# HGRN2's values of all four heads in one 512-column product, computed behind the memory attention

## The chip, the core and the metric

The kernel runs on one core of a Trainium2 chip. A core has five engines that run their own instruction queues side by side: TensorE (PE; its weight loads are shown apart as PEld), VectorE (DVE), ScalarE (ACT), GpSimd (POOL), and SyncE (SP), which here only starts DMA transfers. Each queue is served in order: an instruction that waits holds up all that stand behind it on its engine. The metric is the time of one execution on the device, in microseconds (us), lower is better.

## The reference

One decoder layer over 1024 tokens of width 1024. One projection of the normalised input gives the columns for three groups of heads; their outputs are concatenated, projected, added, and followed by a SwiGLU block.

```python
h = rmsnorm(x, norm_mix[layer])
hq, hf, hi, hg, sq, sk, sv, iq, ik, iw, mq = split_in(h @ w_in[layer])
o_hg = hgrn2_mix(hq, hf, hi, hg, lb[layer], hg_out_gain[layer])        # 4 heads, state 128 x 128
o_sa = dsa_mix(sq, sk, sv, iq, ik, iw, sa_q_gain[layer], sa_k_gain[layer])  # top 256 keys of each query
o_mem = mem_mix(mq, mem_n, w_mem_kv[layer], mem_q_gain[layer], mem_k_gain[layer])  # 256 memory tokens
x = x + jnp.concatenate([o_hg, o_sa, o_mem], -1) @ w_out[layer]
a, b = jnp.split(rmsnorm(x, norm_ffn[layer]) @ w_ffn_in[layer], 2, axis=-1)
x = x + (jax.nn.silu(a) * b) @ w_ffn_out[layer]
```

The change touches `hi`, the values of the gated recurrence: 1024 tokens by 512 columns (4 heads of 128), a product of the normalised input with 1024 x 512 weights.

## The kernel before

Activations lie transposed: 128 channels on the partitions, tokens along the free axis. Every large product is done in float32 accuracy with three passes: both operands are split into a high part (fp32r) and the rest, and high x high, high x low and low x high are added in PSUM (`PASSES`, three pairs). A split of weights is one ACT copy (`whi`) and one subtraction (`wlo`), on POOL in this part of the program.

Weights come in pages of 512 KB, 1024 numbers a partition, through two staging buffers (tag `wst`, two of them for the whole program), and are split from there into tiles of 512 columns (tags `whi`, `wlo`, four of each). A staging buffer is free again when both of its halves are split.

Two shapes of projection stand in this part of the program:

- `proj` (its matmuls are line 184): a page of weights is the stationary operand, 512 tokens move. For a page of 128 outputs: 2 halves of the tokens x 8 slices of the channels x 3 passes = 48 matmuls of 512 columns. The two halves use the two banks of tag `mm`.
- `token_major` (line 453): 128 tokens are the stationary operand and 256 columns of weights move, so that the result has tokens on the partitions. For 256 outputs: 2 pages (each one half of the channels) x 8 tiles of tokens x 12 = 192 matmuls of 256 columns, accumulated in four banks (two of tag `lg`, two of tag `sm`) with two tiles of tokens in each bank; `scaled_rows` (line 462) writes them out with ACT, 8 copies of 128 x 256.

`hgrn_v(pair)` computes the values of two heads with `token_major`. It is called twice: pair 0 first of all, ahead of the memory attention, and pair 1 just before the state of head 1.

The stage around it, from the end of the index scores (about 150 us) to the queries of the sparse attention (about 517 us), holds much independent work at once:

- `memory_attention`: 8 blocks of queries x 2 pairs of heads. Each: logits (PE, line 686), maximum (DVE, 690), exponential (ACT, 693), scaling (POOL, 697), transposes (PE, 702), a copy (ACT 704 or DVE 706), values (PE, 711). It uses the banks `lg`, `rc` and `sm`, its queries `mqs` in x8 to x11, its keys `kms` in x6 and x7 and its values `vm` in x12.
- two searches for the 256th largest score of each query, 32 rounds each, every round one step deeper into the bits of the threshold: `bisect((7, 4), V)` counts on DVE (line 635: 1024 and 640 columns a round), `bisect((6, 5, 3, 2), S)` counts on ACT (line 632: 896, 768, 512 and 384 columns a round) and updates the threshold on DVE (lines 637, 647, 644, 627). A round can't begin before the round ahead of it has ended on DVE. Behind the last round the masks of those blocks are made: counting (657, 667), prefix sums (672) and combination (673, 674) on DVE, comparisons on POOL (669, 675).
- the four heads of the recurrence, for each `hgrn_proj` (3 pages, evacuated by DVE line 481), `hgrn_gates` (ACT lines 493, 495, 496, 501; DVE 494; POOL 497, 498, 502), `hgrn_intra` (six levels of fp32 products, PE line 511, each followed by DVE 521, 523, 535 and POOL 522, then two with line 542) and `hgrn_state` (PE 560, 567, 583, 585, 601).
- pages of queries, keys and values for the sparse attention (names `sap_`).

The program is written as calls in a row (memory attention, head 0, and so on), but a scheduler fixes the order on each engine when the kernel is built: it lists instructions as they become ready in its own timing of the program, within the limits that buffers and banks set. So the static order on PE and DVE interleaves the parts, and it changes wherever the program changes.

Of the kernel before, what the change touches and what calls it, by code (L numbers as in the profile page):

```python
# [42 lines left out]
def hybrid_block(ctx, tc, xT, memT, wch, wikw, wv, wkm, wvm, woa, wob, wfi, wfo,  # L43
                 vec, cst, lvl, out):
    nc = tc.nc
# [14 lines left out]
    def nm(p):  # L60
        cnt[0] += 1
        return f"{ph[0]}_{p}{cnt[0]}"
# [8 lines left out]
    def xt(i, shape, dt=F32):  # L71
        return xp.tile(shape, dt, tag=f"x{i}", name=nm(f"x{i}_"))

    def mt(i, shape=(128, 1024)):
        return mp.tile(list(shape), F32, tag=f"m{i}", name=nm(f"m{i}_"))
# [7 lines left out]
    def bs(b):  # L83
        return slice(b * 128, b * 128 + 128)
# [358 lines left out]
    def token_major(g0):  # L443

        acc = [bank("lg"), bank("lg"), bank("sm"), bank("sm")]
        for g in range(2):
            w = load_page(wv[g0 + g], 4, 256)
            for tt in range(8):
                o = acc[tt // 2][:, 256 * (tt % 2):256 * (tt % 2) + 256]
                i = 0  # L450
                for pw, p in PASSES:
                    for k in range(4):
                        T.matmul(o, H[p][4 * g + k][tt // 4][:, bs(tt % 4)], w(pw, k),
                                 start=g == 0 and i == 0 and tt % 2 == 0,
                                 stop=g == 1 and i == 11 and tt % 2 == 1)
                        i += 1
        return [a.rearrange("p (t d) -> p t d", t=2) for a in acc]

    def scaled_rows(dst, acc):

        for tt in range(8):
            S.activation(dst[tt // 4][:, tt % 4, :], acc[tt // 2][:, tt % 2, :], AF.Copy,
                         scale=rn[:, tt:tt + 1])

    def hgrn_v(pair):
        ph[0] = "hg"
        Vp = [xt(10 + j, [128, 4, 256]) if pair else mt(4 + j, (128, 4, 256)) for j in range(2)]
        scaled_rows(Vp, token_major(2 * pair))
        for j in range(2):
            Vh[2 * pair + j] = lambda c, j=j: Vp[c // 4][:, c % 4, bs(j)]  # L470

    def hgrn_proj(h):
        ph[0] = "hg"
# [131 lines left out]
    def run(steps):  # L605
        ph[0] = "hg"
        for _ in steps:
            pass
# [141 lines left out]

        proj(page(20), 128, H, evac_q0)

    hgrn_v(0)
    memory_attention()
    hgrn_proj(0)
    hgrn_gates(0)
    run(hgrn_intra(0))
    hgrn_proj(1)
    hgrn_gates(1)
    sparse_queries()  # L760
# [1 line left out]
    sparse_values()  # L762
    hgrn_proj(2)
    run(hgrn_intra(1))
    hgrn_v(1)
    run(hgrn_state(1))
    hgrn_gates(2)
    run(hgrn_intra(2))
# [507 lines left out]
```

## Time and profile before

| | us |
|---|---|
| median of 3 runs | 1438.13 |
| lowest and highest | 1438.04, 1438.91 |
| profiled execution | 1437.38 |
| its span, first to last instruction | 1435.6 |
| busy in it: PE, DVE, ACT, POOL | 1331.7, 1062.5, 685.2, 462.4 |

The profile is of one execution. A matmul's busy time includes the time in which it drains beside the next one, so a busy PE isn't PE at its best rate; the pitch, the time from one start to the next in a long uninterrupted run, is what one costs. PE's clock has two levels here, 2.4 and 1.2 GHz; PEclk is the mean granted, 1.00 for the higher one throughout. Times in the rows below count from the start of the span.

### The profile page before, as it was taken

The numbers are of one execution on the slowest core, as the hardware profiler recorded it, in microseconds if no ns is written. First come the engines' busy times: TensorE is split into PE (matmuls) and PEld (weight loads), VectorE is DVE, ScalarE is ACT, GpSimd is POOL, SyncE is SP. The second block draws the span as 40 slices with busy tenths as digits, with TensorE's granted clock in tenths as the row PEclk, the third lists the DMA queues.
The fourth block names the chain that finished last, engine by engine and source line by source line (L and its number), as shares of the span: only waits on it lengthen the run. The fifth ranks groups of instructions, "written<-read, shape, count | busy, mean of one in ns | idle before, by whom it ended". The sixth has DMA issues, their size and how long they took to land.

```text
span 1435.6 us, 19694 instructions
## 1 busy us (share of the span) xinstructions
PE 1331.7 (93%) x6920; PEld 1103.6 (77%) x6920; DVE 1062.5 (74%) x2119; ACT 685.2 (48%) x1350; POOL 462.4 (32%) x380
## 2 busy tenths in 40 slices
PE   7989999989999978999992999999999998899998
PEld 5767887779888867878771788888888886688887
DVE  8787998895496789654489578777777766666764
ACT  7565789857732252544543333333333333344442
POOL 1401034363365533211115133333332310903630
PEclk9999999999999997999995999999999999899999
DMA  6211011000101000011331232323333249543331
GB/s 229 74 30 30 16 45 31 30 22 27 56 17 45 19 18 32 31 34 48 103 118 58 74 109 97 103 102 103 103 110 110 97 138 352 197 165 101 103 110 59
DMA packets 50643, 120.08 MB, mean 84 GB/s; under 512 B 5744, under 2 KB 5872, under 8 KB 50544
## 3 DMA queue, kind: packets, MB, share of 16 engines
q1 hardware_dynamic: 50256, 118.61, 24.8%
q8 instruction: 54, 0.88, 0.3%
q14 instruction: 45, 0.37, 0.1%
q10 hardware_dynamic: 288, 0.22, 0.0%
HBM read 90.23 MB, written 28.57 MB: 83 GB/s over the span
## 4 chain that ended last, share of the span: by engine, by line
PE 64%; DVE 20%; ACT 9%; DMA 3%; issue 2%; POOL 0%; DVEq 0%; ACTq 0%; POOLq 0%; SPq 0%
PE ff_lg L1030 16%; PE ff_rc L1030 12%; PE wo_mm L184 4%; PE fo_mm L1172 4%; PE fo_sm L1172 4%; ACT idx_x L632 4%; PE fo_lg L1172 3%; PE fo_rc L1172 3%; DVE idx_x L635 3%; PE hg_mm L184 2%; PE sap_mm L184 2%; PE wo_mm L1006 2%; PE idx_mm L184 1%; PE mat_mm L184 1%; PE sat_rc L857 1%
## 5 line engine op out<-in xcount | busy, mean ns | idle before, releaser
L115 ACT ACTIVATE ff_whi<-ff_x 128x512 fp32r<-128x512 f32 x109 | 68.4, 630 | 125.7 <-PE ff_rc L1030 80.2
L1030 PE MATMUL ff_lg<-wo_h,ff_whi 128*128 128x512 f32 x440 | 127.0, 394 | 0.0
L632 ACT ACTIVATE idx_x<-idx_x,packs 128x896 int8<-128x896 f32 (+3 forms) x128 | 105.7, 826 | 44.1 <-DVE packs L627 39.4
L1030 PEld LDWEIGHTS ff_lg<-wo_h,ff_whi 128*128 128x128 f32 x440 | 82.5, 189 | 19.6 <-ACT ff_tmp L1036 2.9
L184 PE MATMUL hg_mm<-xn_h,hg_whi 128*128 128x512 f32 x384 | 96.7, 396 | 0.8 <-DVE hg_x L481 0.8
L1030 PE MATMUL ff_rc<-wo_x,ff_whi 128*128 128x512 f32 x264 | 80.9, 392 | 17.2 <-ACT wo_x L115 17.2
L116 DVE TENSOR_TENSOR ff_wlo<-ff_x,ff_whi 128x512 fp32r<-128x512 f32 x109 | 90.6, 832 | 6.4 <-PE ff_lg L1030 4.4
L1030 PE MATMUL ff_rc<-wo_h,ff_whi 128*128 128x512 f32 x264 | 83.4, 397 | 8.9 <-ACT ff_whi L115 6.6
L184 PEld LDWEIGHTS hg_mm<-xn_h,hg_whi 128*128 128x128 f32 x384 | 71.0, 189 | 15.4 <-DVE hg_x L481 1.0
L1030 PE MATMUL ff_lg<-wo_x,ff_whi 128*128 128x512 f32 x264 | 78.8, 391 | 0.0
L116 POOL TENSOR_TENSOR hg_wlo<-hg_wst,hg_whi 128x512 fp32r<-128x512 f32 x32 | 43.0, 1352 | 104.8 <-ACT hg_whi L115 79.1
L1030 PEld LDWEIGHTS ff_rc<-wo_x,ff_whi 128*128 128x128 f32 x264 | 49.8, 189 | 28.1 <-ACT wo_x L115 17.7
L635 DVE TENSOR_SCALAR_CACHE_REDUCE idx_x<-idx_x,packs 128x1024 int8<-128x1024 f32 x64 | 68.7, 1074 | 0.9
L1030 PE MATMUL ff_lg<-wo_h,ff_wlo 128*128 128x512 f32 x220 | 67.8, 389 | 0.0
L1030 PEld LDWEIGHTS ff_rc<-wo_h,ff_whi 128*128 128x128 f32 x264 | 50.2, 190 | 20.5 <-ACT ff_whi L115 7.0
L511 PE MATMUL hg_rc<-hg_x,hg_x 128*128 128x128 f32 x384 | 53.0, 289 | 11.2 <-POOL hg_x L522 5.7
L511 PEld LDWEIGHTS hg_rc<-hg_x,hg_x 128*128 128x128 f32 x384 | 49.4, 202 | 15.5 <-POOL hg_x L522 7.8
L522 POOL TENSOR_TENSOR hg_x<-hg_x,hg_x 128x256 f32<-128x256 f32 x56 | 45.4, 822 | 43.8 <-PE hg_rc L511 27.1
L1030 PEld LDWEIGHTS ff_lg<-wo_x,ff_whi 128*128 128x128 f32 x264 | 49.7, 188 | 10.7 <-ACT ff_whi L115 0.2
L836 POOL TENSOR_SCALAR sat_x<-sat_x,sat_mz 128x1024 f32<-128x1024 f32 (+7 forms) x32 | 24.1, 755 | 99.6 <-DVE sat_mz L835 80.1
L384 DVE SCALAR_TENSOR_TENSOR idx_x<-idx_tmp,packs,idx_x 128x512 f32<-128x512 f32 (+2 forms) x70 | 46.1, 711 | 12.3 <-ACT idx_tmp L379 11.9
L116 DVE TENSOR_TENSOR fo_wlo<-fo_tmp,fo_whi 128x512 fp32r<-128x512 f32 x33 | 33.5, 1017 | 26.4 <-ACT fo_whi L115 23.7
(445 smaller groups left out, 3722.6 us busy)
## 6 DMA issues: line engine op xcount, KB each, us to landing
gd<-ff_m SPq DMA_DIRECT2D x77, 256.0 KB, 2.0
fo_x<-gd SPq DMA_DIRECT2D x77, 256.0 KB, 3.0
ff_wst<-wfi SPq DMA_DIRECT2D x16, 512.0 KB, 3.6
ff_m<-wfi SPq DMA_DIRECT2D x14, 512.0 KB, 3.6
ff_x<-wfi SPq DMA_DIRECT2D x14, 512.0 KB, 3.7
hg_wst<-wch SPq DMA_DIRECT2D x12, 512.0 KB, 3.6
fo_x<-wfo SPq DMA_DIRECT2D x12, 512.0 KB, 6.4
fo_h<-wfo SPq DMA_DIRECT2D x20, 256.0 KB, 6.0
```

Source lines behind the costliest of these rows:

```text
L115: S.activation(hi, src, AF.Copy)
L116: (eng or V).tensor_sub(lo, src, hi.bitcast(F32))
L184: T.matmul(ps[:M, :], w(pw, k), h[p][k][hf], start=i == 0, stop=i == len(order) - 1)
L384: V.scalar_tensor_tensor(sc[b][:, c0:c1], rl[:, :c1 - c0], iww[:, b, h:h + 1], sc[b][:, c0:c1], op0=ALU.mult, op1=ALU.add)
L511: T.matmul(rc[:, bs(c)], K[:, bs(4 * hf + c)], Q[:, bs(4 * hf + c)], start=True, stop=True)
L522: G.tensor_mul(Kv[:, :, 0, :], Kv[:, :, 0, :], fr.to_broadcast([128, n, w]))
L632: S.activation(waste[S][:, :nk], sc[b], AF.Sign, bias=nf[:, j:j + 1], accum_out=ct[:, j:j + 1])
L635: eng.tensor_scalar(waste[eng][:, :nk], sc[b], fl[:, j:j + 1], None, op0=ALU.is_ge, op1=ALU.add, accum_out=ct[:, j:j + 1])
L836: G.tensor_scalar(P[:, :nk], P[:, :nk], mx[:, 2:3], 1.0, op0=ALU.mult, op1=ALU.mult)
L1006: T.matmul(ps, wb[k](pw, m), MX[p][KB[k]][hf], start=i == 0, stop=i == 8)
L1030: T.matmul(ps, w[pw][:, bs(k)], HB[u][k][p], start=first and i == 0, stop=i == 11, skip_group_check=True)
L1172: T.matmul(banks[m], w[i][pw][:, bs(m)], b[i][p], start=first and i == 0 and n == 0, stop=i == NP - 1 and n == 2, skip_group_check=True)
```

## The change

`hgrn_v` computes all four heads in one go: 512 columns of weights move for each stationary tile of 128 tokens, in place of 256. A bank holds one tile of tokens, so the four banks hold 512 tokens, and the two halves of the channels (`g`) can't stay in PSUM for both halves of the tokens (`th`): for `g = 0` ACT writes the partial sums out, and for `g = 1` DVE adds the second half to them. It is called once, behind the memory attention and the first steps of head 0.

```diff
-    def hgrn_v(pair):
+    def hgrn_v():
         ph[0] = "hg"
-        Vp = [xt(10 + j, [128, 4, 256]) if pair else mt(4 + j, (128, 4, 256)) for j in range(2)]
-        scaled_rows(Vp, token_major(2 * pair))
-        for j in range(2):
-            Vh[2 * pair + j] = lambda c, j=j: Vp[c // 4][:, c % 4, bs(j)]
+        Vp = [[mt(4 + j, (128, 4, 256)) for j in range(2)],
+              [xt(10 + j, [128, 4, 256]) for j in range(2)]]
+        for g in range(2):
+            st = [wp.tile([128, 1024], F32, tag="wst", name=nm("wst"), bufs=2) for _ in range(2)]
+            for pair in range(2):
+                nc.sync.dma_start(st[pair], wv[2 * pair + g])
+            w = []
+            for k in range(4):
+                if g == 0:
+                    t = xt((6, 7, 12, 9)[k], [128, 1024], F32R)
+                    t = t[:, :512], t[:, 512:]
+                else:
+                    t = [wp.tile([128, 512], F32R, tag=i, name=nm(i)) for i in ("whi", "wlo")]
+                for pair in range(2):
+                    c = slice(256 * pair, 256 * pair + 256)
+                    split(t[0][:, c], t[1][:, c], st[pair][:, 256 * k:256 * k + 256],
+                          lo_engine[0])
+                w.append(t)
+            for th in range(2):
+                acc = [bank(t) for t in ("lg", "lg", "sm", "sm")]
+                steps = [(tt, pw, p, k) for tt in range(4) for k in range(4) for pw, p in PASSES]
+                if g and th:
+                    steps.sort(key=lambda t: t[3])
+                n = [0] * 4
+                for tt, pw, p, k in steps:
+                    T.matmul(acc[tt], H[p][4 * g + k][th][:, bs(tt)], w[k][pw],
+                             start=n[tt] == 0, stop=n[tt] == 11)
+                    n[tt] += 1
+                for tt in range(4):
+                    r = rn[:, 4 * th + tt:4 * th + tt + 1]
+                    for pair in range(2):
+                        o = Vp[pair][th][:, tt, :]
+                        ps = acc[tt][:, 256 * pair:256 * pair + 256]
+                        if g == 0:
+                            S.activation(o, ps, AF.Copy, scale=r)
+                        else:
+                            V.scalar_tensor_tensor(o, ps, r, o, op0=ALU.mult, op1=ALU.add)
...
-    hgrn_v(0)
     memory_attention()
     hgrn_proj(0)
     hgrn_gates(0)
     run(hgrn_intra(0))
+    hgrn_v()
     hgrn_proj(1)
...
     run(hgrn_intra(1))
-    hgrn_v(1)
     run(hgrn_state(1))
```

The split weights of `g = 0` go into x6, x7, x12 and x9, which hold keys, values and queries of the memory attention until its last block. Lines of the new kernel stand 35 or 36 further down than the same lines before (686 is 722, 511 is 547); the new product is line 493.

The scheduler's order moves far beyond the lines that were edited. On PE, in the second half of the memory attention, the order before holds matmuls of head 1's pages (`hg_mm`, line 184) between the products of the attention (`mat_`):

```order
L686 MATMUL mat_lg_2250<-mkv_x_114_576,mat_x_339_1433 128x256 x2
L702 MATMUL mat_rc_2186<-packs,mat_m_382_1858 128x128 x2
L686 MATMUL mat_lg_2250<-mkv_x_114_576,mat_x_340_1434 128x256 x2
L702 MATMUL mat_rc_2186<-packs,mat_m_382_1858 128x128 x2
L184 MATMUL hg_mm_2670<-xn_h_176,hg_whi_2640 128x512
L184 MATMUL hg_mm_2670<-xn_h_180,hg_whi_2640 128x512
L184 MATMUL hg_mm_2670<-xn_h_184,hg_whi_2640 128x512
L184 MATMUL hg_mm_2670<-xn_h_188,hg_whi_2640 128x512
L702 MATMUL mat_rc_2212<-packs,mat_m_382_1858 128x128 x2
```

On PE at the same place of the new program only the attention's own products are left:

```order
L738 MATMUL mat_rc_1856<-packs,mat_m_366_1632 128x128 x2
L722 MATMUL mat_lg_1920<-mkv_x_114_576,mat_x_339_1433 128x256 x2
L722 MATMUL mat_lg_1920<-mkv_x_114_576,mat_x_340_1434 128x256 x2
L738 MATMUL mat_rc_1882<-packs,mat_m_366_1632 128x128 x2
L747 MATMUL mat_sm_1862<-mat_m_367_1633,mkv_x_115_577 64x128 x4
L738 MATMUL mat_rc_1882<-packs,mat_m_366_1632 128x128 x2
L722 MATMUL mat_lg_1946<-mkv_x_113_575,mat_x_337_1431 128x256 x2
```

Between the end of the index scores and the last product of the attention, the order before has 297 matmuls of line 184 and 192 of line 453; the new one has 192 of line 184, none of 453 and the first 12 of line 493. All of head 1's pages have moved behind the attention.

On DVE, where the masks of the second search are made, the order before has steps of head 1's `hgrn_intra` (521, 535, 523) between steps of the masks (657 to 667); three of its six levels stand ahead of this piece:

```order
L657 TENSOR_SCALAR idx_x_156_802,packs<-idx_x_157_803,packs 128x384
L521 TENSOR_TENSOR hg_x_505_2630<-hg_x_505_2630,hg_x_507_2632 128x32x8
L535 COPY_PREDICATED hg_x_530_2820<-packs,hg_rc_3484 128x512
L659 TENSOR_SCALAR packs<-packs 128x4
L523 TENSOR_TENSOR hg_x_507_2632<-hg_x_507_2632 128x32
L662 TENSOR_TENSOR packs<-packs 128x4
L663 TENSOR_TENSOR packs<-packs 128x4
L667 TENSOR_SCALAR idx_x_156_802,packs<-idx_x_155_801,packs 128x896
```

On DVE in the new order that head's first step (563, 564, which were 527 and 528) comes when the masks (703 to 710, which were 667 to 674) are nearly done, and its levels stand behind all of them:

```order
L563 TENSOR_TENSOR hg_x_525_2700<-hg_x_525_2700,hg_x_527_2702 128x512
L564 TENSOR_TENSOR hg_x_550_2890<-hg_rc_3491,packs 128x512
L703 TENSOR_SCALAR idx_x_156_802,packs<-idx_x_157_803,packs 128x384
L706 TENSOR_SCALAR packs<-packs 128x1
L708 SCALAR_TENSOR_TENSOR idx_x_157_803<-idx_x_158_804 128x384
L709 SCALAR_TENSOR_TENSOR idx_x_157_803<-idx_x_157_803,packs,idx_x_158_804 128x384
L710 SCALAR_TENSOR_TENSOR idx_x_157_803<-idx_x_156_802,idx_x_157_803 128x384
L557 TENSOR_TENSOR hg_x_525_2700<-hg_x_525_2700,hg_x_527_2702 128x256
```

The piece from the first 657 to the first copy of head 1's state (572) now holds all of `hgrn_intra(1)` and four evacuations of head 2's pages that stood ahead of it. Behind that copy the next 189 rows of DVE are the same in both orders.

On PE, the levels of head 1 (511) stood before between matmuls of the second pair's values (453):

```order
L511 MATMUL hg_rc_3430<-hg_x_505_2630,hg_x_506_2631 128x128 x4
L453 MATMUL hg_lg_3566<-hg_whi_3571,xn_h_127 128x256
L453 MATMUL hg_lg_3566<-hg_whi_3571,xn_h_131 128x256
L453 MATMUL hg_lg_3566<-hg_whi_3575,xn_h_135 128x256
L453 MATMUL hg_lg_3566<-hg_whi_3575,xn_h_139 128x256
L511 MATMUL hg_rc_3435<-hg_x_505_2630,hg_x_506_2631 128x128 x4
```

On PE in the new order the last three levels (547), the two steps behind them (578) and the state (596 and on) follow each other with nothing between:

```order
L184 MATMUL hg_mm_3921<-xn_h_187,hg_wlo_3892 128x512
L547 MATMUL hg_rc_3536<-hg_x_525_2700,hg_x_526_2701 128x128 x4
L547 MATMUL hg_rc_3541<-hg_x_525_2700,hg_x_526_2701 128x128 x4
L547 MATMUL hg_rc_3554<-hg_x_525_2700,hg_x_526_2701 128x128 x4
L547 MATMUL hg_rc_3559<-hg_x_525_2700,hg_x_526_2701 128x128 x4
L547 MATMUL hg_rc_3572<-hg_x_525_2700,hg_x_526_2701 128x128 x4
L547 MATMUL hg_rc_3577<-hg_x_525_2700,hg_x_526_2701 128x128 x4
L578 MATMUL hg_rc_3590<-hg_x_525_2700,hg_x_526_2701 32x32 x16
L578 MATMUL hg_rc_3615<-hg_x_525_2700,hg_x_526_2701 64x64 x8
L596 MATMUL hg_rc_3634<-packs,hg_x_526_2701 128x128 x4
```

From the 48 matmuls of head 3's second page, which follow head 1's state in both, the two orders on PE are alike again up to the sparse attention, in which some products change places.

## Rows read from the trace of the kernel before

**Rows 1.** Page, busy times, share of the span and instructions of each engine
```profile
PE 1331.7 (93%) x6920; PEld 1103.6 (77%) x6920; DVE 1062.5 (74%) x2119; ACT 685.2 (48%) x1350; POOL 462.4 (32%) x380
```

**Rows 2.** Stretches: us, busy (instructions) of each engine, PEclk, DMA share, GB/s
```profile
core 0: us, PE busy (x) PEld busy (x) DVE busy (x) ACT busy (x) POOL busy (x), PEclk, DMA share, GB/s
154.70:285.30 130.60, 124.99 (x778) 103.27 (x778) 119.73 (x356) 111.68 (x263) 43.64 (x58) 1.00 0.11 33
156.70:278.90 122.20, 116.67 (x720) 95.80 (x719) 111.67 (x337) 105.62 (x248) 40.08 (x55) 1.00 0.10 31
279.60:447.70 168.10, 155.45 (x1081) 140.81 (x1079) 126.96 (x300) 97.28 (x212) 85.19 (x72) 0.98 0.12 35
285.30:404.10 118.80, 110.09 (x747) 99.72 (x746) 81.45 (x208) 82.61 (x182) 52.23 (x45) 0.99 0.11 32
404.80:442.40 37.60, 34.39 (x260) 31.07 (x260) 35.76 (x65) 9.35 (x19) 28.13 (x22) 0.95 0.10 29
447.70:517.40 69.70, 69.65 (x429) 60.21 (x430) 47.91 (x136) 18.33 (x33) 25.83 (x26) 1.00 0.08 23
530.00:550.00 20.00, 11.00 (x37) 8.85 (x38) 19.46 (x59) 11.34 (x19) 4.37 (x4) 0.55 0.21 69
```

**Rows 3.** Chain that ended last: start us, us, engine, tile, line, instructions
```profile
150.88 4.90 PE hg_lg L453 x41
...
468.85 4.55 PE hg_mm L184 x20
```

**Rows 4.** DVE, 156.7 to 278.9, groups: count | busy us, mean ns | idle before
```profile
L635 DVE TENSOR_SCALAR_CACHE_REDUCE idx_x<-idx_x,packs 128x1024 int8<-128x1024 f32 x27 | 34.5, 1276 | 0.5
L635 DVE TENSOR_SCALAR_CACHE_REDUCE idx_x<-idx_x,packs 128x640 int8<-128x640 f32 x27 | 23.5, 872 | 0.2
...
L644 DVE SCALAR_TENSOR_TENSOR packs<-packs 128x2 int32<-128x2 int32 x26 | 6.6, 253 | 0.2
...
L481 DVE TENSOR_TENSOR hg_x<-hg_mm,rrow 128x512 f32<-128x512 f32 x7 | 4.8, 682 | 0.0
```

**Rows 5.** ACT, 285.3 to 404.1, groups by shape
```profile
L632 ACT ACTIVATE idx_x<-idx_x,packs 128x896 int8<-128x896 f32 x17 | 17.7, 1041 | 25.4 <-DVE packs L627 25.4
...
L632 ACT ACTIVATION_READ_ACCUMULATOR idx_x<-idx_x,packs 128x1 f32 x69 | 12.9, 188 | 0.0
...
L115 ACT ACTIVATE hg_whi<-hg_wst 128x512 fp32r<-128x512 f32 x10 | 5.9, 620 | 0.0
...
L462 ACT ACTIVATE sap_x<-sap_sm,packs 128x256 f32<-128x256 f32 x4 | 1.7, 467 | 0.0
```

**Rows 6.** ACT by time: first counts of successive rounds of the second search
```profile
363.50 1.04 ACT L632 ACTIVATE idx_x<-idx_x,packs 128x896 int8<-128x896 f32 x1 [0.90 <-DVE packs L627]
...
368.94 1.04 ACT L632 ACTIVATE idx_x<-idx_x,packs 128x896 int8<-128x896 f32 x1 [0.37 <-DVE packs L627]
...
374.10 1.04 ACT L632 ACTIVATE idx_x<-idx_x,packs 128x896 int8<-128x896 f32 x1
```

**Rows 7.** DVE, whole span, groups of the recurrence and of line 384 by shape
```profile
L481 DVE TENSOR_TENSOR hg_x<-hg_mm,rrow 128x512 f32<-128x512 f32 x16 | 10.8, 684 | 2.8 <-PE hg_mm L184 2.4 <-PE hg_rc L585 0.4
...
L527 DVE TENSOR_TENSOR hg_x<-hg_x,hg_x 128x512 f32<-128x512 f32 x8 | 5.5, 685 | 1.3 <-PE hg_rc L511 1.3
...
L523 DVE TENSOR_TENSOR hg_x<-hg_x 128x256 f32<-128x256 f32 x8 | 3.6, 449 | 0.0
...
L384 DVE SCALAR_TENSOR_TENSOR idx_x<-idx_tmp,packs,idx_x 128x256 f32<-128x256 f32 x7 | 3.4, 479 | 0.2 <-ACT idx_tmp L379 0.2
...
L384 DVE SCALAR_TENSOR_TENSOR idx_x<-idx_tmp,packs,idx_x 128x128 f32<-128x128 f32 x7 | 2.4, 343 | 0.0
```

**Rows 8.** DVE, 390 to 442.4, groups by shape
```profile
L521 DVE TENSOR_TENSOR hg_x<-hg_x,hg_x 128x256 f32<-128x256 f32 x14 | 7.7, 549 | 0.0
L535 DVE COPY_PREDICATED hg_x<-packs,hg_rc 128x512 f32<-128x512 uint8 x10 | 7.4, 736 | 0.0
```

**Rows 9.** Line 511, what PE waited for before it: us, times
```profile
  POOL hg_x L522: 13.5, 6
```

More of the change, by code (lines that the diff above doesn't have):

```diff
@@ L463, in scaled_rows @@
                          scale=rn[:, tt:tt + 1])
-    def hgrn_v(pair):
+    def hgrn_v():
         ph[0] = "hg"
-        Vp = [xt(10 + j, [128, 4, 256]) if pair else mt(4 + j, (128, 4, 256)) for j in range(2)]
-        scaled_rows(Vp, token_major(2 * pair))
-        for j in range(2):
-            Vh[2 * pair + j] = lambda c, j=j: Vp[c // 4][:, c % 4, bs(j)]
+        Vp = [[mt(4 + j, (128, 4, 256)) for j in range(2)],
[35 more added lines that the diff above has]
+                            V.scalar_tensor_tensor(o, ps, r, o, op0=ALU.mult, op1=ALU.add)
+        for h in range(4):
+            Vh[h] = lambda c, v=Vp[h // 2], j=h % 2: v[c // 4][:, c % 4, bs(j)]
```

## The prediction

> **What bounds the kernel now.** I read the busy line of the page first [rows 1]: PE is busy for 1331.7 of 1435.6 us, no other engine for more than 74%. That is a mean, so next I read stretches around the edited code [rows 2]. The stage from about 150 to 517 us falls into three pieces. From 156.7 to 278.9 the memory attention runs, and PE, DVE and ACT are all nearly full there (DVE 111.67 and ACT 105.62 of 122.2 us). From 285.3 to 404.1 DVE has 37.4 us idle and ACT 36.2, while the second search goes on, round by round; ACT waits for line 627 of DVE for 25.4 us ahead of 17 rounds, 1.5 us a round [rows 5]. From 404.8 to 442.4 DVE is full (35.76 of 37.6): the masks and the last levels of head 1. Over 279.6 to 447.7 PE has 155.45 us of work in 168.1, so 12.65 idle. Behind 447.7 PE is busy 69.65 of 69.7 us: whatever is late at 447.7 is late at the end. So I forecast how far this point moves, the 48 matmuls of head 3's second page behind head 1's state, which both orders have.
>
> **The product itself.** In the chain of waits 41 matmuls of line 453 (256 columns) take 4.90 us, 119.5 ns each, and 20 of line 184 (512 columns) take 4.55 us, 227.5 ns each [rows 3]. The change takes out 384 of the first kind, 45.9 us, and adds 192 of the second, 43.7 us. It saves 2.2 us of PE, because twice the columns cost nearly twice the time.
> The Trainium skill ("TensorE: Matmul & The Clock Gate", section "Back-to-back issue gap") gives about 131 ns for a matmul of 512 columns in a sustained stream of weight loads and matmuls. By it the 192 would cost 25.2 us, an estimate from that page, and the change would save 20.7 us; the trace does not agree, its 227.5 ns decide.
>
> **The edits around it.** The splits of the weights become 16 copies of 256 columns on ACT in place of 8 of 512: 16 x 0.31 (half of 620 ns) to 16 x 0.467 us against 8 x 0.620 [rows 5], so 0 to 2.5 us more on ACT; I take 1, lying in ACT's waits. POOL has the same number of subtractions, at the same widths, and is 32% busy. The partial sums go out with 16 copies on ACT, as many as before, and 16 additions on DVE are new: the nearest row, the same operation of 256 columns on line 384, takes 479 ns and of 128 columns 343 [rows 7], so 5.5 to 7.7 us; I take 7.7. They fall between 285 and 404, where DVE has 37.4 us free. Each waits for a bank of PE's product, and behind it on DVE may stand line 627, for which ACT waits; with that cover gone the price is 7.7. The four loads of 512 KB stay four (DMA share 0.11 there); but they take both staging buffers, and SP holds all pages queued behind them.
>
> **What moves: the memory attention loses its fillers.** The two staging buffers are asked for by the new product, whose first half can only be split into x6, x7, x12 and x9 when the attention has left them. Until then no page of head 1 can be loaded. So 105 matmuls of line 184 (297 less 192) and 192 of line 453 leave the attention, 12 of the new product and about 1.8 us of fp32 products of head 0 come in. PE work pushed behind it: 105 x 0.2275 + 192 x 0.1195 - 12 x 0.2275 - 1.8 = 42.3 us; less the 2.2 saved, 40 us more for PE behind the attention.
> What the attention gains is set by DVE, its fullest engine besides PE. By the new order these leave the piece [rows 4]: 5 counts of 1024 (1.276) and 4 of 640 (0.872), 9.9 us; 3 of line 481, 2.0; two of line 494, which I price at the 0.685 of another 128x512 operation [rows 7], 1.4; some 24 small steps of thresholds at 0.253, 6.1; two of 0.685 come in, -1.4. Together 18.0 us. With DVE's idle time as before (10.5 us) the piece ends at 278.9 - 18.0 = 260.9. If none of the idle stays it is 250.4; if the chain of products, maxima and exponentials keeps 7 us more idle, 268. I take 261, since the chain of each block is the same as before, and 262 for PE's last product. ACT gets rid of 12 copies of 512 (7.4 us), 8 of line 462 (3.7) and 14 counts; a count is 1.041 us at 896 columns, at the mean of 640 some 0.74, with its read of 0.188 some 0.93 [rows 5], so 13.0: together 24.1 us.
>
> **PE's route to the point.** From 262 PE has 155.45 + 40 = 195.4 us of work, so it is there at 457.4 with no idle time, +10 us. With all of the 12.65 us idle kept it is 470, +22; with half, 463.7, +16. The waits before the point (search, masks, head 1) stay, but 40 us of free matmuls can fill some of them: I take half.
>
> **DVE's and ACT's route.** In the new order 11.25 rounds of the second search are done at the end of the attention, 14.75 before, so 20.75 are left in place of 17.25. A round with little beside it takes 5.2 to 5.4 us [rows 6]. ACT's work behind 261: the 82.6 of the stretch 285.3 to 404.1, 6.4 for the time from 278.9 to 285.3 if full, and the 24.1 pushed there, 113.1; with 1.5 us of waiting in each of 20.75 rounds, 31.1, the search ends at 405, against 404 before. Were the pushed copies to hide a third of those waits it is 395; by the whole pace of before, (404.1 - 278.9)/17.25 = 7.26 us a round, 412. So 17 us gained by the attention are used up here.
> Behind it comes the full piece of DVE. In the new order it holds, besides what it held, two each of lines 527 and 528 (0.685, both 128x512), four of 521 (0.549), four of 535 (0.736), four of 523 (0.449) and four of 481 (0.684) [rows 7, 8]: 2.7 + 2.2 + 2.9 + 1.8 + 2.7 = 12.4 us. Head 1's last levels now also follow each other on PE with nothing between. Where line 511 waited for POOL's line 522, it was 13.5 us in 6 waits, 2.25 each [rows 9]; three levels in a row make up to 6.7 us, some of it beside the DVE work already counted. I take 4, between 2 and 6. The piece becomes 37.6 + 12.4 + 4 = 54 us, and with the 5.3 us from 442.4 to 447.7 the point comes at 405 + 54 + 5.3 = 464.3, +16.6.
>
> **Sum.** The two routes end at +16 and +16.6; I take +16. The work behind the point is the same but for products that change places in the sparse attention, which I put at 0, within 5 us either way. The profiled execution took 1437.38 us; 1437.4 + 16 = 1453.4, and the median of the runs lies 0.75 above the profiled one: **1454 us**. The bounds, with the ends of both routes (+10 and +22, at 395 +6.6, at 412 +23.6) and those 5 us, are +3 to +28, 1441 to 1466.
>
> **Rivals.** *The attention runs at DVE's floor (faster).* It ends at 250.4, PE's last product there at 251.4, and PE then has next to no gaps. Its busy time counts fill and drain too: by the pitches [rows 3] and the order's counts, the work of the 155.45 us packs into some 147, an estimate. So 251.4 + 147 + 40 + 2 us idle = 440, -7.5, **1430**. It decides once the attention ends by 251 and PE then idles under 8 us in 190. For it: three engines share the work more evenly. Against it: PE idled 12.65 us in the same calls, and the round-by-round search can't be shortened by free PE work.
> *The displaced matmuls fill idle time only (no change).* If they take all of PE's 12.65 us idle, the attention ends at 255 and the levels of head 1 run ahead of the last round, 255 + 195.4 = 450 less some 2 us of pipelining: **1438**. Against it: DVE's order puts those levels behind the masks.
> *PE loses its clock in the attention.* Counted by the new order and priced as above, PE has about 35 us of work in the last 77 us of it. Before, from 530 to 550 us, PE was busy 11.00 of 20 us and its granted clock was 0.55 [rows 2], near the lower of its two levels, 1.2 GHz. At 0.55 those 35 us take 64, which still fits into 77, but each block's chain passes through PE three times; I take a tenth of the 77 us, +8 us: **1462**. Against it: the work doesn't pause for long, it is thin.
> *A matmul costs by the piece and not by the column,* so that the product is worth what its name says: 192 x 119.5 ns, 22.9 us, saves 20.7 more than my sum: **1433**. The skill's section above would point this way. Against it: the 227.5 ns of 512 columns on the same engine [rows 3].
>
> **Chances.** About 0.2%, 2.9 us, is what a measurement of this kernel can tell from no change. Forecast (1441 to 1466) 0.67; clock lost 0.18, slower too; DVE's floor 0.08; no change 0.06; cost by the piece 0.01. That makes faster 0.09, no change 0.06, slower 0.85. The range runs from 1438, which leaves out the two faster cases, to 1472, which takes in the clock on top of the upper half of my bounds.
>
> **What would show it.** In the profile of the new kernel: line 493 at about 227 ns from start to start (right) or near 130 (wrong by the product). The last products of the attention at 262 us and a busy share of PE that falls towards there, with the granted clock beside it; if it ends at 250, the gain is larger than I say. The last count of the second search at 405. From the first 693 (657 before) to head 1's 608 (572 before) 54 us; 40 would mean that the levels found cover. Head 3's second page at 464 in place of 447.7. Should PE still be full from 262 to the point and this come by 450, the forecast fails by its idle time; should the difference at the end not be the difference at that point, it fails by the tail.

## The result and the profile after

The changed kernel takes 1471.39 us (median of 4 runs, 1470.15 to 1474.37) against 1438.09 before: a ratio of 1.0235, 95% interval [1.0223, 1.0247], 33.3 us slower. 1454 was forecast: the direction was right, the shift is twice the forecast one, and the time lies at the upper end of the range. The profiled execution took 1471.99 us, its span is 1470.2.

Busy times of the page of the changed kernel, which answer to [rows 1]:

```profile
PE 1346.0 (92%) x6728; PEld 1103.3 (75%) x6728; DVE 1071.4 (73%) x2135; ACT 687.0 (47%) x1358; POOL 467.2 (32%) x388
```

PE has 192 matmuls fewer, as planned, and is busy for 14 us more. No engine is fuller than before; the time went into stretches in which PE waited or ran slowly. By stretches, for comparison with [rows 2]:

```profile
core 0: us, PE busy (x) PEld busy (x) DVE busy (x) ACT busy (x) POOL busy (x), PEclk, DMA share, GB/s
155.50:261.30 105.80, 87.05 (x491) 67.11 (x489) 91.10 (x294) 86.01 (x207) 30.17 (x48) 0.91 0.04 11
...
240.00:261.30 21.30, 12.64 (x76) 8.90 (x74) 12.94 (x39) 18.20 (x39) 10.00 (x14) 0.76 0.00 1
261.30:474.20 212.90, 198.40 (x1158) 171.79 (x1156) 150.86 (x359) 118.70 (x262) 99.48 (x86) 0.96 0.13 40
340.00:380.00 40.00, 34.42 (x199) 31.02 (x198) 12.13 (x41) 33.16 (x73) 13.06 (x12) 0.87 0.13 41
412.40:469.60 57.20, 49.00 (x290) 40.94 (x289) 50.43 (x86) 9.57 (x17) 44.03 (x34) 0.94 0.12 37
441.00:474.20 33.20, 27.82 (x204) 23.97 (x204) 29.93 (x60) 4.89 (x9) 20.22 (x21) 0.90 0.11 33
474.30:543.90 69.60, 69.60 (x429) 60.19 (x430) 47.86 (x136) 18.27 (x33) 25.86 (x26) 1.00 0.08 22
567.10:736.30 169.20, 159.08 (x960) 126.46 (x960) 107.86 (x337) 75.84 (x169) 37.79 (x48) 0.95 0.13 39
```

The attention ends at 261.3 in place of 279.6. In its last 21.3 us the DMA share is 0.00, so no page of weights is loaded there, and ACT is the fullest engine (18.20 us busy, DVE 12.94). The chain that ended last runs on ACT there, through loads of its function tables (the pieces without a tile, 1.28 us each) and the exponentials between them, until the first matmuls of the new product (start, us):

```profile
240.90 1.28 ACT L729
...
243.90 1.28 ACT L537
...
254.82 1.90 PE hg_lg L493 x7
```

From the attention's end to the point behind head 1's state, PE has 198.40 us of work in 212.9: 14.5 us idle, more than the 12.65 of before, and parts of it at a lower clock (0.87 from 340 to 380, 0.90 in the last levels of head 1). The point comes at 474.3, 26.5 us later than the 447.8 of before. Behind it 429 matmuls again fill PE without a gap: the stretch of 69.6 us is the one of 69.65 in [rows 2]. The last row is the sparse attention, 169.2 us; before it was:

```profile
540.60:703.10 162.50, 155.71 (x959) 126.53 (x959) 103.03 (x337) 75.43 (x167) 37.12 (x48) 0.95 0.13 39
```

So 26.5 us are lost up to the point, 6.6 in the sparse attention, and 1.5 behind it.

The waits of PE from 261 to 474 (engine and line, what it waited for: us, times, longest):

```profile
PE sap_sm L399 <- ACT sap_tmp L396: 5.6, 1, 5.6
PE hg_rc L547 <- DVE hg_x L563: 3.9, 1, 3.9
PE hg_rc L547 <- DVE hg_x L557: 1.6, 3, 1.2
PE hg_rc L578 <- DVE hg_x L557: 1.4, 2, 0.8
```

Nearly 7 us are waits of head 1's levels for DVE (557 and 563 were 521 and 527); the other wait, 5.6 us at once, is for squares that ACT makes between the counts of the search. This is the last part of the chain that ended last (start, us):

```profile
397.47 20.89 PE hg_mm L184 x92
420.08 2.56 POOL hg_x L534
...
429.70 2.30 POOL hg_x L534
...
444.88 1.77 DVE idx_x L708
```

It runs on PE, with pages of the recurrence, until 418.4; then on POOL, whose comparisons for the masks stand between the gates of head 2 (lines 533, 534 and 538, which were 497, 498 and 502); then on DVE, with the masks and head 1's levels. From 418.4 to 437.2 POOL is busy 18.55 of 18.80 us. The end of the search, 411.1, is not on this chain. No run here changes POOL's part alone, so its share of the loss isn't shown.

The product itself, PE in order of time (start, us for the group, idle time ahead in brackets):

```profile
299.63 0.39 PE L493 MATMUL hg_sm<-hg_wlo,xn_h 128*128 128x512 f32 x1
299.86 0.62 PE L493 MATMUL hg_sm<-hg_whi,xn_h 128*128 128x512 f32 x2
300.31 0.39 PE L493 MATMUL hg_sm<-hg_wlo,xn_h 128*128 128x512 f32 x1
300.54 0.62 PE L493 MATMUL hg_sm<-hg_whi,xn_h 128*128 128x512 f32 x2
300.99 0.39 PE L493 MATMUL hg_sm<-hg_wlo,xn_h 128*128 128x512 f32 x1
```

From 299.63 to 300.99 six matmuls start, one in 227 ns, as line 184's did in [rows 3].

### The profile page after: what moved, and what is told of

It is laid out like the page before. It is cut to its first block, busy times and chain, and to the rows that moved or that the text cites. A ratio compares the mean times of both kernels' runs of the same rounds, so it can differ in the third digit from the quotient of the medians.

```text
span 1470.2 us, 19338 instructions
## 1 busy us (share of the span) xinstructions
PE 1346.0 (92%) x6728; PEld 1103.3 (75%) x6728; DVE 1071.4 (73%) x2135; ACT 687.0 (47%) x1358; POOL 467.2 (32%) x388
## 4 chain that ended last, share of the span: by engine, by line
PE 67%; DVE 20%; ACT 8%; issue 2%; DMA 2%; POOL 1%; DVEq 0%; ACTq 0%; POOLq 0%; SPq 0%
PE ff_lg L1065 16%; PE ff_rc L1065 12%; PE fo_mm L1207 4%; PE fo_sm L1207 4%; PE wo_mm L184 4%; PE hg_mm L184 3%; PE fo_lg L1207 3%; PE fo_rc L1207 3%; DVE idx_x L671 3%; ACT idx_x L668 2%; PE sap_mm L184 2%; PE wo_mm L1041 2%; PE idx_mm L184 1%; DVE idx_x L384 1%; PE sat_mm L892 1%
## 5 line engine op out<-in xcount | busy, mean ns | idle before, releaser
L116 POOL TENSOR_TENSOR hg_wlo<-hg_wst,hg_whi 128x512 fp32r<-128x512 f32 (+1 forms) x32 | 42.0, 1329 | 100.6 <-ACT hg_whi L115 65.8
L1065 PEld LDWEIGHTS ff_lg<-wo_x,ff_whi 128*128 128x128 f32 x264 | 49.9, 189 | 10.5
```

The lines of the kernel that those rows point to most:

```text
L116: (eng or V).tensor_sub(lo, src, hi.bitcast(F32))
L1065: T.matmul(ps, w[pw][:, bs(k)], HB[u][k][p], start=first and i == 0, stop=i == 11, skip_group_check=True)
```

## The experiments

All readings of the traces together. "Point" is the first matmul of head 3's second page behind head 1's state; "sparse" is the length of the sparse attention, from its first logits to its last values. Each ratio is against runs of the kernel before made on the same chip with it. The columns behind the ratio are from one profile each. The changed kernel, e8 and e11 have the same order up to the point, and so have e10 and its two variants below: their points lie up to 1.2 and 2.8 us apart, so a smaller difference of two points says nothing.

| kernel | time, us | ratio, 95% interval | attention ends | search ends | point | sparse |
|---|---|---|---|---|---|---|
| before | 1438.09 | 1 | 279.6 | 404.0 | 447.8 | 162.6 |
| changed | 1471.39 | 1.0235 [1.0223, 1.0247] | 261.3 | 411.1 | 474.3 | 169.2 |
| e1 old products, new place | 1464.31 | 1.0179 [1.0163, 1.0194] | 259.9 | 405.1 | 473.7 | 162.3 |
| e2 head 1's pages first | 1457.19 | 1.0127 [1.0112, 1.0142] | 279.7 | 411.3 | 464.5 | 164.9 |
| e3 two halves of 256 | 1473.03 | 1.0237 [1.0220, 1.0254] | 265.9 | 415.5 | 479.7 | 166.8 |
| e5 head 1's levels early | 1454.08 | 1.0104 [1.0089, 1.0119] | 263.5 | 414.6 | 460.7 | 163.9 |
| e6 e2 and e5 | 1442.25 | 1.0032 [1.0020, 1.0044] | 278.1 | 411.6 | 448.0 | 164.0 |
| e7 e6, all sums in the banks | 1444.39 | 1.0045 [1.0031, 1.0059] | 278.6 | 413.2 | 451.0 | 164.1 |
| e10 e6 with the old products | 1440.40 | 1.0009 [1.0000, 1.0018] | 276.0 | 400.5 | 441.0 | 166.0 |
| e12 e6 without the additions | 1439.55 | 1.0013 [1.0003, 1.0023] | 279.8 | 405.5 | 446.6 | 165.3 |
| e15 changed, without the additions | 1472.18 | 1.0241 [1.0224, 1.0258] | 261.0 | 406.0 | 476.7 | 168.0 |
| e8 changed, head 3 earlier | 1474.03 | 1.0249 [1.0233, 1.0265] | 262.5 | 412.3 | 475.2 | 171.4 |
| e11 e8 with the pages kept | 1465.34 | 1.0188 [1.0166, 1.0210] | 262.8 | 412.6 | 475.5 | 162.2 |

**The place or the product?** e1 is the kernel before with both calls moved:

```diff
-    hgrn_v(0)
     memory_attention()
...
     run(hgrn_intra(0))
+    hgrn_v(0)
+    hgrn_v(1)
     hgrn_proj(1)
...
     run(hgrn_intra(1))
-    hgrn_v(1)
```

> The kernel before, with its own 256-column products for both pairs, called one after the other at the new place behind the first steps of head 0. Theory A (the place and the two staging buffers cost, since head 1's pages leave the memory attention: its order holds 192 matmuls of line 184 there, as the changed kernel's does, and 63 of the values): 1462 to 1476 us. Rival B (the merged form costs: partial sums, 16 additions on DVE, four banks held): 1438 to 1448 us.

With the old products at the new place the point comes at 473.7, 0.6 us from the changed kernel. The loss up to the point belongs to the place; the merged form adds nothing to it there. What e1 is faster by, 7 us, lies behind the point: its sparse attention takes 162.3 us.

**What 512 columns are worth.** e3 issues each merged matmul as two of 256:

```diff
-                    T.matmul(acc[tt], H[p][4 * g + k][th][:, bs(tt)], w[k][pw],
-                             start=n[tt] == 0, stop=n[tt] == 11)
+                    for c in range(2):
+                        cs2 = slice(256 * c, 256 * c + 256)
+                        T.matmul(acc[tt][:, cs2], H[p][4 * g + k][th][:, bs(tt)], w[k][pw][:, cs2],
+                                 start=n[tt] == 0 and c == 0, stop=n[tt] == 11 and c == 1)
```

> The changed kernel, with every merged matmul of 512 columns issued as two of 256. By the pitches of the kernel before (119.5 and 227.5 ns) PE gets 2.2 us more work: 1471 to 1475 us. If a matmul costs by the piece, 192 more cost some 23 us: 1485 to 1495.

It takes 1473.03 us, 1.6 more than the changed kernel; the intervals of the two ratios overlap. This agreement of the whole times is partly chance: the attention ends 4.6 us later, the point comes 5.4 us later, and the sparse attention is 2.4 us shorter. But from the attention's end to the point PE is busy for 200.50 us, 2.1 more than in the changed kernel, and a longer run of its halves in the chain of waits (start, us, instructions) has one matmul in 120 ns:

```profile
303.59 5.76 PE hg_sm L495 x48
```

So 192 matmuls more cost PE about the 2.2 us of the pitches and not some 23, and a matmul here costs by its columns. The merging saves what the two pitches say, about 2 us of PE.

**The displaced pages.** e2 calls head 1's pages ahead of the product, so that they are first at the staging buffers:

```diff
-    hgrn_v()
     hgrn_proj(1)
+    hgrn_v()
     hgrn_gates(1)
```

> The changed kernel, with head 1's three pages called ahead of the merged product, so that 336 matmuls of line 184 stand in the memory attention (297 before, 192 after the change); head 1's levels still stand among the masks on DVE. If PE's displaced work sets the time (33 us of it come back): 1445 to 1455 us. If the chain of search, masks and head 1's levels sets it, a later end of the attention eats the gain: 1462 to 1472 us. If the fillers are without effect and the merged form costs: 1469 to 1473.

**Head 1's levels.** e5 leaves the product in its new place, and calls the levels of head 1 behind its gates:

```diff
     hgrn_gates(1)
+    run(hgrn_intra(1))
     sparse_queries()
...
     hgrn_proj(2)
-    run(hgrn_intra(1))
     run(hgrn_state(1))
```

> The changed kernel, with the levels of head 1 called directly behind its gates, so that none of them stands among the masks on DVE any more (24 more steps stand there in the changed kernel than before). If the piece of masks and levels sets the time: 57 us become about 42, 1456 to 1462 us. If PE's displaced work sets it: 1466 to 1472.

Both gain, by different means. With e2 the attention ends at 279.7 again, and the point comes 9.8 us earlier than in the changed kernel: the 18 us that the attention had won are given back, and PE has 29 us less to do behind it. With e5 the attention stays short (263.5), and the point comes 13.6 us earlier. PE from the attention's end to the point, first e2, then e5 (columns as above):

```profile
279.70:464.50 184.80, 169.09 (x1022) 148.00 (x1020) 130.06 (x315) 102.76 (x231) 86.27 (x76) 0.93 0.13 38
...
263.50:460.70 197.20, 192.56 (x1153) 167.67 (x1152) 145.87 (x357) 118.64 (x261) 95.09 (x85) 0.98 0.13 41
```

e2 still has 15.7 us idle and a clock of 0.93, since head 1's levels stand alone on PE: 9.3 us of its waits are of line 547 for POOL, between 429 and 446. In e5 4.6 us are idle, and from 415.3 on, behind the search, PE is busy without a gap up to the point: there PE's amount of work sets the point. The times were both missed by the forecasts made for them. e2 lies 2 us above what PE's displaced work gave and 5 below what the chain of masks gave; e5 lies 2 us below what the piece of masks gave and 12 below what PE's displaced work gave. So each cause is one part of the loss.

**Both edits.** e6 is e2 and e5 in one.

> The changed kernel with both edits: head 1's pages ahead of the merged product, and its levels directly behind its gates. Theory A (two separate losses: PE work displaced from the memory attention, and head 1's levels piled among the masks): the point behind head 1's state moves from 474 us in the changed kernel to 448 to 452, the time to 1437 to 1446 us. If the two edits recover the same idle time, it stays at that of the better one alone: 1451 to 1455.

The point is at 448.0 us, where it is in the kernel before, 26.3 us earlier than in the changed kernel; the two edits alone gave 9.8 and 13.6. So the two edits undo the whole loss up to the point. 4 us are left in the time. (The old products gain more from the same two edits, as e10 below shows.)

**The additions.** e12 is e6, and e15 the changed kernel, without the sixteen additions:

```diff
                         if g == 0:
                             S.activation(o, ps, AF.Copy, scale=r)
-                        else:
-                            V.scalar_tensor_tensor(o, ps, r, o, op0=ALU.mult, op1=ALU.add)
```

> The kernel with both edits, without the 16 additions of the second half's partial sums on DVE (the values then lack the second half of the channels). With the additions the second search ends at 411.6 us and the point behind head 1's state comes at 448.0; with the old products in the same place at 400.5 and 441.0. If the additions hold up the search's steps behind them on DVE: search at 400 to 405, point at 439 to 443. If the merged form is late for another reason (weights that can't be split before the attention's end): 409 to 412 and 446 to 449.

> The changed kernel without the 16 additions of the second half's partial sums on DVE (the values then lack the second half of the channels). In the changed kernel the second search ends at 411.1 us where 405 was forecast with the additions in idle time, and the point comes at 474.3. If the additions held up the search: it ends at 404 to 406, the point at 467 to 470. If the search is late by its own pace: 410 to 412 and 473 to 475.

In both the search ends 5 to 6 us earlier, at 405.5 and 406.0; 405 was forecast for the changed kernel with the additions in idle time. They weren't in idle time: in the changed kernel they run from 295 to 322, in a stretch in which masks and counts of the first search keep DVE nearly full (25.34 of 27.3 us). There ACT, in order of time (idle time ahead and its cause in brackets), waits for a step of the threshold that stands behind them:

```profile
313.43 0.63 ACT L115 ACTIVATE hg_whi<-hg_wst 128x512 fp32r<-128x512 f32 x1 [1.38 <-PE hg_sm L493]
322.23 1.04 ACT L668 ACTIVATE idx_x<-idx_x,packs 128x896 int8<-128x896 f32 x1 [8.17 <-DVE packs L663]
```

and this is DVE in that wait, in which it has no idle time (masks of the first search take most of it, six additions 2.4 us):

```profile
318.18 0.47 DVE L504 SCALAR_TENSOR_TENSOR hg_m<-hg_lg,packs,hg_m 128x256 f32<-128x256 f32 x1
...
320.88 0.47 DVE L504 SCALAR_TENSOR_TENSOR hg_m<-hg_sm,packs,hg_m 128x256 f32<-128x256 f32 x1
321.28 0.47 DVE L504 SCALAR_TENSOR_TENSOR hg_x<-hg_sm,packs,hg_x 128x256 f32<-128x256 f32 x1
321.67 0.47 DVE L663 TENSOR_SCALAR packs<-packs 128x4 int32<-128x4 int32 x1
```

Yet the earlier search is worth nothing in the changed kernel: e15's point comes at 476.7, and 1472.18 us is its time. The piece from the first mask count to head 1's state grows from 57.2 to 65.3 us; PE has 197.80 us of work before the point there as well. Part of this is the order: the masks are done 5 us earlier, but in e15's order head 1's first step (563 in the changed kernel) stands behind the last of them on DVE, in the changed kernel ahead of it, so that its levels begin at 447.2 us, against 448.0. Both forecasts came out split: in e12 and e15 the search ends as if the additions held it up, and the point comes as if they didn't. In e6's place the additions cost 2.7 us of the time by the medians (the two intervals just overlap). e7 takes them away in another way: the split weights of both halves stay, and all 24 matmuls of a bank add up in it.

```diff
...
-                steps = [(tt, pw, p, k) for tt in range(4) for k in range(4) for pw, p in PASSES]
+            steps = [(tt, pw, p, k) for g in range(2) for tt in range(4)
+                     for k in range(4 * g, 4 * g + 4) for pw, p in PASSES]
...
```

> The kernel with both edits, in which both halves of the channels also add up in the banks (the split weights of both stay in place), so that the 16 additions on DVE are gone and ACT writes each value once. If the additions on DVE lie in idle time, within 2 us of that kernel: 1436 to 1447. If they delay the search behind them on DVE: 5 to 8 us less than it.

It is no better than e6 (1444.39 against 1442.25): the search ends at 413.2 although the additions are gone, so as much is lost elsewhere. The runs don't show where.

**The old products in the mended place.** e10 has e6's calls and the old function, called twice.

> The kernel with both edits, but with the old 256-column products of the two pairs in the place of the merged one; the orders stand alike otherwise (336 matmuls of line 184 and 24 of 453, where the merged one has 12 of 493, in the memory attention). By the pitches the merged product saves 2.2 us, and the additions lie in idle time: 1442 to 1447 us against 1442. If the merged form costs something of its own (partial sums, additions): 1434 to 1440.

The time, 1440.40 us, lies between the two forecasts. At the point e10 is 7 us ahead of e6 (441.0), and 6.8 ahead of the kernel before; 3.3 us of it are lost from the point to the sparse attention (96.2 us in place of 92.8) and 3.4 in the sparse attention (166.0), so that the time is that of before. Two variants, e13 and e14, have other steps ahead of the sparse attention; they gave 1439.41 (ratio 1.0003) and 1438.91 (1.0002), no difference from the kernel before either. Their points, 443.9 and 443.6, are 4 us ahead of it and of e6. So in the order of e6 the merged form costs some 4 to 7 us up to the point, which it didn't at the changed place (e1). How much of it the additions are isn't shown: e12's point, 446.6, is too close to e6's.

> The kernel with both edits and the old products, with three filling steps of head 3 ahead of the sparse attention and the output projection's pages kept in their place by three empty steps. It is at the point 6.8 us before the kernel before, and loses that again up to the end of the sparse attention. If the place of head 3's steps loses it: 1432 to 1436 us. If not: 1438 to 1441.

> The same with one filling step ahead and three empty steps, so that some matmuls of the output projection's pages move behind the sparse attention (2.5 us of work by the pitches). If later pages keep PE filled to the end of the sparse attention: 1432 to 1437 us. If they are missed inside it: 1440 to 1444.

**The sparse attention.** In the changed kernel PE waits in the middle of it, in a stretch where DVE is nearly full; at the same place of the kernel before, which comes 26.5 us earlier there, PE was full at the higher clock. First the changed kernel, then the kernel before:

```profile
647.10:657.10 10.00, 7.74 (x36) 6.30 (x36) 9.06 (x30) 5.25 (x12) 3.53 (x5) 0.66 0.00 1
```

```profile
620.60:630.60 10.00, 10.00 (x58) 8.08 (x58) 3.90 (x15) 3.92 (x9) 1.60 (x2) 1.00 0.18 52
```

The order differs there: head 3's last level stands behind 32 matmuls of logits on PE, behind 20 before. The pages of the output projection, which are the fillers, come later: before, nearly all of them are spread from the 60th to the 80th matmul of logits; in the changed kernel only two stand ahead of the 70th. e8 calls four of the filling steps ahead:

```diff
     rest = fillers()
+    for _ in range(4):
+        next(rest)
     for _ in sparse_attention():
```

> The changed kernel, with the first four of the steps that fill the sparse attention (three of head 3's levels among them) called ahead of it. In the changed kernel's order head 3's last level stands behind 32 of the sparse attention's logits on PE (20 before), its state comes late, and the sparse attention takes 169.2 us (162.6 before). If that order costs the 6.6 us: its stretch 162 to 165 us, the time 1464 to 1468. If the sparse attention is slow for another reason: 1470 to 1473.

It made it longer, 171.4 us: the pages moved forward with head 3, and none stands among the last 28 matmuls of logits. The same edit cost the kernel before 7 us (b2: 1444.84 against 1437.99; its sparse attention takes 168.6 in place of 162.6) and e6 about 4 (e9: 1446.05; 169.1 in place of 164.0).

> The kernel before, with the first four filling steps of head 3 called ahead of the sparse attention. If the place of head 3 among the sparse attention's products still costs there: 1433 to 1437 us. If not: 1437 to 1439.

> The kernel with both edits, and the first four filling steps of head 3 ahead of the sparse attention. If an earlier state of head 3 fills the sparse attention better than its order does now (164.0 us): 1437 to 1441. If that order is as good as before's: 1441 to 1444.

e11 calls three of them ahead, and puts three empty steps ahead of the pages, so that these stay where they were before:

```diff
...
+        for _ in range(3):
+            yield
         po_tag[0] = "rc"
...
     rest = fillers()
+    for _ in range(3):
+        next(rest)
     for _ in sparse_attention():
```

> The changed kernel, with the first three filling steps of head 3 ahead of the sparse attention and three empty steps behind head 3's state, so that the pages of the output projection stand among the sparse attention's products as they do in the kernel before; head 3's last level still stands behind 28 logits (32 in the changed kernel, 20 before). If the order of the pages towards the end makes the sparse attention long: 162 to 165 us for it, 1464 to 1467 in all. If head 3's late levels do: 167 to 169, 1469 to 1472.

The sparse attention takes 162.2 us, and the kernel 1465.34, 6 us less than the changed one. Head 3's last level is hardly earlier in it (28 matmuls of logits ahead of it, as in e8), and the pages lie as before, so the order of the pages sets this length, not head 3's level. It is a matter of the scheduler's listing: e1, whose products stand at the same place, got the good order.

**The kernel before with e5's edit.** b1 takes 1439.27 us, ratio 1.0007 [0.9999, 1.0016]: neither forecast was met, and moving head 1's levels gains nothing there.

> The kernel before, with the one edit that the levels of head 1 are called directly behind its gates; its masks hold 26 fewer steps of them. If the masks' piece on DVE set the time of the kernel before as well: 1428 to 1434 us. If PE's work did (12.65 us idle in 168, of which some 6 lie in waits for these levels): 1432 to 1437.

Its search ended 2.9 us earlier (401.1), and its point came 2.4 us later (450.2). No version here beat the kernel before.

## Why the prediction was half right

The direction and the mechanism were right: the attention loses its fillers, and PE has their work to do behind it. Two steps failed, and together they double the loss: that half of PE's idle time would be filled, and that nothing would change behind the point.

- *The product saves 2 us only:* this was right. A matmul of 512 columns takes 227 ns and one of 256 takes 120, and e3 gives PE 2.1 us more work.
- *The attention loses its fillers and ends at 261 (DVE), 262 (PE):* it ended at 261.3, but that the number fits so well is partly luck. DVE's work in it fell by 20.6 us (from 111.67 to 91.10) and not by 18.0, its idle time grew from 10.5 to 14.7 us in place of staying, and the stretch began 1.2 us earlier. Towards the end it was ACT's chain that set the pace, not DVE.
- *PE has 195.4 us of work from there to the point:* it was 198.4, and the 3 us more are PE's clock. At the lower of its levels PE was busy for 13.0 us (from 358.9 to 369.1 and from 440.8 to 447.7, at 0.50 and 0.51), before for 6.75 us (from 323.9 to 327.3 and from 426.3 to 429.7, at 0.50). At the higher level they would have taken half as long (an estimate), so the clock cost 6.5 us in place of 3.4.
- *"I take half" of PE's idle time, 6.3 us:* this step failed. 14.5 us were idle, more than the whole of before. The argument was that 40 us of free matmuls fill waits. But the order puts these matmuls ahead of head 1's levels and leaves the levels alone, and they waited for 6.9 us; 5.6 us more are the one wait for ACT's squares. e5, which moved only the levels, has 4.6 us idle and a clock of 0.98 in place of 0.96. With 3 us for the clock and 8.2 us more idle time, the PE route's 463.7 becomes 474.9, less the 0.7 of the attention 474.2: where the point is.
- *The search ends at 405:* it ended at 411.1, near the bound by the pace of before. The additions took 0.47 us each, as priced, but they were taken to lie in idle time because DVE had 37.4 us free there before, and they hit a full piece of that stretch; without them the search ends at 406.0. So the lost cover cost 5 to 6 us, for which 7.7 had been named. But it wasn't on the path: the chain passes from PE's pages to POOL, and e15's point isn't earlier.
- *The masks with head 1's levels take 54 us, and 5.3 to the point:* they took 57.2 and 4.7. This is right in kind, and it is the part of the loss that e5 takes away. DVE's work in the piece was 50.43 us where 48.2 were priced; some steps of head 1 took longer than the rows they were priced by (685 and 449 ns in [rows 7]), for a reason that no run shows:

```profile
L563 DVE TENSOR_TENSOR hg_x<-hg_x,hg_x 128x512 f32<-128x512 f32 x2 | 2.4, 1214 | 0.0
...
L559 DVE TENSOR_TENSOR hg_x<-hg_x 128x256 f32<-128x256 f32 x2 | 2.2, 1098 | 0.0
```

- *The two routes agree:* that was no proof. One took PE's idle time to be filled and the other DVE's, and neither was. No route passed through POOL, on which the chain lies from 418.4 to 437.
- *Behind the point nothing changes, within 5 us:* this step failed too. 6.6 us were lost in the sparse attention and 1.5 behind it. The order there was known to differ, and was priced at zero; e11 shows that it was worth 6. The 1.5 us stay open and may be chance: this last part took 732.5 to 734.6 us in the other kernels here, also without a merged product (in e14, which moves pages there, 735.4).
- *The rivals:* PE's clock did fall in the attention (0.76 over its last 21.3 us, with PE busy 12.64), but the attention ended on time: the forecast price of 8 us wasn't paid there. Behind the attention a lower clock cost the 3 us above. That a matmul costs by the piece and not by the column is refuted by e3. That the attention runs at DVE's floor, or that only idle time is refilled, is refuted by its end at 261.3, not 250 to 255, and by the idle time, which grew.

The sum in the forecast's own terms: 16 us were forecast; 10.5 more at the point (8.2 idle, 3.0 slow, -0.7) and 8.1 behind it give 34.6, the difference of the two spans (1470.2 - 1435.6).

## What to carry to other kernels

Where a step is moved, first ask what stood in the queue of its buffers behind it: here two staging buffers passed from head 1's pages to a product that couldn't start, and some 42 us of fillers left a stage that needed them. Work on a full engine is not enough to fill its waits; see in the order whether a chain with waits has independent work between its links, since here the chain that stood alone paid each wait and a lower clock besides. Where the order of the fillers is known to change, as in the sparse attention here, it should not be priced at zero: it was worth 6 us. And cost an edit's small operations at the place where the new order puts them, stretch by stretch, then ask separately whether the delay reaches the end: in the changed kernel it didn't.

## What was not expected of the hardware

PE's clock fell to 0.76 of full speed in the last 21.3 us of the attention, where PE was busy 12.64 us, and the end of that stretch wasn't delayed: the chain that ended last ran on ACT there. In the 10 us of the sparse attention in which PE was busy 7.74, the clock was 0.66. There PE first waited for DVE, and then the lower clock counted: from 650.1 to 655.7 us the chain that ended last is PE alone, at a granted clock of 0.50. What that level costs can be read from head 1's levels: eight matmuls of line 547 took 2.08 us at 441.3, where the clock was 0.51, and 1.13 us at 453.8, where it was 1.00.
